# Weight sums of a seven-product scheme: two of four made by adding transfers, in another order of products

## The chip, the cores and the metric

The kernel runs on one core of a Trainium2 chip. The metric is the device time of one execution in microseconds. TensorE (PE) does the matrix products, VectorE (DVE) and ScalarE (ACT) the elementwise work, GpSimd (POOL) has so far little to do, and SyncE (SP) issues the transfers.

## The reference, cut to what matters

One decoder layer runs on 512 prompt tokens and 64 sample tokens (576 in all, model width 2048):

```
c = rms_norm(x) @ w_in                      # 2048 x 10312: q, k, v, z_attn, indexer, GLU, z_conv, two gates
attn -> branch_attn = (attn * silu(z_attn)) @ w_up_attn          # 1024 x 2048
u = glu_val * sigmoid(glu_gate); dw = depthwise_conv(u, 31 taps)
conv_out = silu(layer_norm(dw)) @ w_pw + b_pw
branch_conv = (conv_out * silu(z_conv)) @ w_up_conv              # 1024 x 2048
merged = sigmoid(gate_attn) * branch_attn + sigmoid(gate_conv) * branch_conv
y = rms_norm(x + merged @ w_out)
```

All data is float32. The change lies in how a part of `x @ w_in` and the whole of `attn @ w_up_attn` are multiplied.

## The kernel before

**Split products.** A float32 weight tile is split by `split` (L160) into a rounded high part (ACT, `whi`, L164) and the rest (DVE, `wlo`, L166). Activations are kept as such two parts too, and each product takes three matmuls: high by high, high by low, low by high. `whi` and `wlo` have three buffers each, so the splits run up to three tiles ahead of PE.

**Plain blocks.** `block` (L238) makes one strip of 128 output channels for all 576 tokens.

**Pairs with seven products.** `strassen` (L169) makes two strips at once, ca and cb. The contraction is cut in two halves, the 576 tokens in two halves of 288, and the two strips are the two halves of the outputs: a two-by-two scheme in which seven products take the place of eight. The weight quarters are b11 (first half of the rows, strip ca), b12 (first half, cb), b21 and b22 (second half). The weight operands are b11, t1 = b12 - b11, t2 = b22 - t1, b22, b21, b22 - b12 and b21 - t2, each of which goes through `split`. The activation operands (A11, A12, A22, S1 to S4) are made once per stage: L944 to L964 for x, L1081 to L1107 for the attention. The order of products is A11, S1, S2, S4, A12, S3, A22. The results are added up from PSUM by DVE into four kept tiles (`sk`), and `ev` gets each finished quarter.

There are 20 pairs with `w_in` (contraction 2048, so quarter tiles of 128x1024; L982, L992, L998), and 8 with `w_up_attn` (contraction 1024, tiles of 128x512; L1135). One pair has 7 x 24 or 7 x 12 matmuls of 288 columns.

**Buffers.** b11 and b12 come from tag `wraw` (two buffers, shared with the plain blocks), b21 and b22 from `wx` (two), t1 and t2 from `wt` (two). One pair thus fills every buffer of the three tags.

**Order of the work.** The order on each engine is not the source's: a planner simulates the engines with its own costs when the kernel is built and takes, of what it thinks is ready, the lowest priority level (`pri`): weight loads, sums and splits 0, evictions 1, preparation and normalisation 3, convolution taps 5, products 6. Each engine and each queue then runs its list in order and waits where an operand is late. SP's queue has the loads and stores; POOL's queue issues only gathers, and POOL computes small scalings and differences, all before 560 us.

**Stages.** Attention, indexer and plain blocks of `w_in` run up to about 660 us; the 20 pairs of `w_in` up to 1120, with the depthwise convolution's taps (L725) and the layer norm (L1012) beside them on DVE; then the plain blocks of `w_pw` and the first pairs of `w_up_attn`; then pairs and plain blocks of `w_up_conv` by turns; and last `w_out` with the final norm.

Of the kernel before, what the change touches and what calls it, by code (L numbers as in the profile page):

```python
# [9 lines left out]
F32 = mybir.dt.float32  # L10
# [4 lines left out]
OP = mybir.AluOpType  # L15
# [70 lines left out]
def build(tc, I, O):  # L86
    nc = tc.nc
    v, s, g, pe = nc.vector, nc.scalar, nc.gpsimd, nc.tensor
    dma = nc.sync.dma_start
# [3 lines left out]
    @contextmanager  # L93
    def pri(level):
        old = tc.cur_priority
        start = level * 1000000 + count.get(level, 0)
        tc.cur_priority = start
        yield
        count[level] = count.get(level, 0) + tc.cur_priority - start
        tc.cur_priority = old  # L100

    def ap(h, off, dims):
        return bass.AP(tensor=h.tensor, offset=h.offset + off, ap=[list(d) for d in dims])

    per = ctx.enter_context(tc.tile_pool(name="per", bufs=1))
# [54 lines left out]
    def split(raw, n=128):  # L160

        k = raw.shape[1]
        hi = per.tile([128, 8, 128], R, name="whi", tag="whi", bufs=3)[:, :k, :n]
        s.copy(hi, raw[:, :, :n])  # L164
        lo = per.tile([128, 8, 128], R, name="wlo", tag="wlo", bufs=3)[:, :k, :n]
        v.tensor_sub(lo, raw[:, :, :n], hi.bitcast(F32))  # L166
        return hi, lo

    def strassen(pool, w, width, ca, cb, A, ev, kts=16, lvl=6, EV=1, rp=None):  # L169


        n = kts // 2
        with pri(0):
            raws = []
            for c0, half, tag in ((ca, 0, "wraw"), (cb, 0, "wraw"), (ca, 1, "wx"), (cb, 1, "wx")):
                t = (per.tile([128, 8, 128], F32, name="wraw", tag="wraw", bufs=2) if tag == "wraw" else
                     (rp or pool).tile([128, 8, 128], F32, name="wx", tag="wx", bufs=2))[:, :n]
                dma(t, ap(w, half * n * 128 * width + c0, [[width, 128], [128 * width, n], [1, 128]]))
                raws.append(t)
            b11, b12, b21, b22 = raws  # L180
            t1 = pool.tile([128, n, 128], F32, name="t1", tag="wt", bufs=2)
            t2 = pool.tile([128, n, 128], F32, name="t2", tag="wt", bufs=2)

        def product(raw, x):
            p = ps.tile([128, 512], F32, name="mms", tag="mm", bufs=4)[:, :T2]
            with pri(0):
                hi, lo = split(raw)
            with pri(lvl):
                for k in range(n):
                    for j, (a, part) in enumerate(((hi, 0), (hi, 1), (lo, 0))):  # L190
                        pe.matmul(p, a[:, k], A[x](part, k), start=(k == 0 and j == 0), stop=(k == n - 1 and j == 2))  # L191
            return p

        def kept():
            return pool.tile([128, T2], F32, name="sk", tag="sk", bufs=5)

        k1, k5, u2, v2 = (kept() for _ in range(4))

        def add(out, a, b):
            with pri(EV):  # L200
                v.tensor_add(out, a, b)  # L201

        p = product(b11, "A11")
        with pri(EV):
            s.copy(k1, p)  # L205
        with pri(0):
            v.tensor_sub(t1, b12, b11)
        p = product(t1, "S1")
        with pri(EV):
            s.copy(k5, p)  # L210
        with pri(0):
            v.tensor_sub(t2, b22, t1)
        p = product(t2, "S2")
        add(u2, p, k1)
        p = product(b22, "S4")
        with pri(0):
            v.tensor_sub(b22, b22, b12)
        add(v2, u2, k5)
        add(v2, p, v2)
        with pri(EV):  # L220
            ev(0, 1, v2)
        p = product(b21, "A12")
        with pri(0):
            v.tensor_sub(b21, b21, t2)
        add(k1, p, k1)
        with pri(EV):
            ev(0, 0, k1)
        p = product(b22, "S3")
        add(u2, p, u2)
        add(k5, u2, k5)  # L230
        with pri(EV):
            ev(1, 1, k5)
        p = product(b21, "A22")
        add(u2, p, u2)
        with pri(EV):
            ev(1, 0, u2)

    def block(w, width, c0, x, n=128, kts=16, lvl=6, hs=(0, 1), units=None):  # L238

        p = {h: ps.tile([128, 512], F32, name=f"mm{h}", tag="mm", bufs=4) for h in hs}  # L240
        for u in range(kts // 8):
            hi, lo = units[u] if units else weight_unit(w, width, c0, n, u * 8)
            with pri(lvl):
                for k in range(8):
                    kt = u * 8 + k
                    for j, (a, part) in enumerate(((hi, 0), (hi, 1), (lo, 0))):
                        for h in hs:
                            pe.matmul(p[h][:n, :HN[h]], a[:, k, :n], x(part, kt, h),  # L248
                                      start=(kt == 0 and j == 0), stop=(kt == kts - 1 and j == 2))
        return p  # L250
# [29 lines left out]
    def xrows(i):  # L280
        return (ap(I["x_prompt"], i * 128 * D, [[D, 128], [1, D]]) if i < 4
                else ap(I["x_sample"], 0, [[D, 64], [1, D]]))

    with tc.tile_pool(name="p0", bufs=1) as p0, pri(-1):
# [11 lines left out]
        def load(i):  # L296
            for cs in (slice(0, D // 2), slice(D // 2, D)):
                dma(xt[i][:TILES[i][1], cs], xrows(i)[:, cs])  # L298
# [27 lines left out]
        for h, tiles in enumerate(((0, 1), (2, 3, 4))):  # L326
            for i in tiles:
                n = TILES[i][1]
                for k, (eng, c0, c1) in enumerate(SQ[i]):
                    x, out = xt[i][:n, c0:c1], ss[:n, i, k:k + 1]  # L330
# [7 lines left out]
            with pri(-2):  # L338
# [13 lines left out]
                for c0, c1, eng in SCALE if h else ():  # L352
                    for k, i in enumerate(tiles):
                        x = xt[i][:TILES[i][1], c0 * 128:c1 * 128]
                        n = TILES[i][1]
                        (g if eng == "P" else v).tensor_scalar(x, x, rr[:n, k:k + 1], rt[:n, k:k + 1],
                                                               op0=OP.mult, op1=OP.mult)
            for kt in range(16):
                tag = PT_TAGS[h][kt % len(PT_TAGS[h])]
                pt = ps.tile([128, 512], F32, name="pt", tag=tag, bufs={"mm": 4, "w": 3, "o": 1}[tag])  # L360
                for i in tiles:
                    t0, n = TILES[i]
# [12 lines left out]
        for q in range(4):  # L375
            rows = slice(q * 32, (q + 1) * 32)
# [12 lines left out]
    CH, TK, EV = 3, 5, 1  # L389
# [31 lines left out]
    p = block(I["w_in"], D_IN, C_KI, xin, 72, units=units)  # L421
# [12 lines left out]
    with pri(CH):  # L434
# [15 lines left out]
        wt = p1.tile([128, 4, 8], F32, name="wt", tag="qh", bufs=2)  # L450
# [17 lines left out]
    for c in range(4):  # L468
        p = ps.tile([128, 512], F32, name="mm1", tag="mm", bufs=4)
# [8 lines left out]
        with pri(EV):  # L478
            s.copy(qi[:, c], p[:, NW:NQ])
            for e in range(2):  # L480
                rows = slice(e * 64, (e + 1) * 64)
# [107 lines left out]
    for kv in range(2):  # L589
        p = win(C_K + 128 * kv)  # L590
# [9 lines left out]
    for kv in range(2):  # L600
        p = win(C_V + 128 * kv)
# [15 lines left out]
    for h in range(NH):  # L617
        p = win(C_Q + 128 * h)
# [318 lines left out]
    def whole(dst, q, c):  # L937
        v.tensor_add(dst, q.bitcast(F32)[:, 0, c], q.bitcast(F32)[:, 1, c])
# [5 lines left out]
    with pri(CH):  # L944
        for q in range(4):
            c = slice(2 * q, 2 * q + 2)
            fs = [p4.tile([128, 2, T2], F32, name="f", tag="f", bufs=4) for _ in range(4)]
            whole(fs[0], quarter(1, 0), c)
            whole(fs[1], quarter(1, 1), c)
            v.tensor_add(fs[1], fs[0], fs[1])  # L950
            whole(fs[2], quarter(0, 0), c)
            parts(s1, fs[1], c)
            v.tensor_sub(fs[2], fs[1], fs[2])
            whole(fs[3], quarter(0, 1), c)
            parts(s2, fs[2], c)
            v.tensor_sub(fs[3], fs[3], fs[2])
            parts(s4, fs[3], c)
        for q in range(4):
            c = slice(2 * q, 2 * q + 2)
            f0, f1 = (st("f").rearrange("p (k t) -> p k t", k=2) for _ in range(2))  # L960
            whole(f0, quarter(0, 0), c)
            whole(f1, quarter(1, 0), c)
            v.tensor_sub(f0, f0, f1)
            parts(quarter(1, 0), f0, c)  # L964
# [47 lines left out]
    with pri(CH):  # L1012
        ones = p5.tile([128, 128], F32, name="ones")
        v.memset(ones, 1.0 / 1024)
        for h in range(2):
            sl, n = TS2[h], T2
# [42 lines left out]
        for k in range(0, 8, 2):  # L1059
            for h, x in ((0, back), (1, dw)):  # L1060
                t = x[:, k:k + 2]
# [19 lines left out]
    with pri(CH):  # L1081
        for k in range(4):
            t1, t2 = st("al"), st("al")
            dma(t1, a_d[k])
            dma(t2, a_d[k + 4])
            x11, x21, x12, x22 = t1[:, TS2[0]], t1[:, TS2[1]], t2[:, TS2[0]], t2[:, TS2[1]]

            def put(name, src):
                o = UA[name]
                s.copy(o[:, 0, k], src)  # L1090
                v.tensor_sub(o[:, 1, k], src, o.bitcast(F32)[:, 0, k])

            def new():
                return pU.tile([128, T2], F32, name="sk", tag="sk", bufs=5)

            f1, f2, f3, f4 = (new() for _ in range(4))
            put("A11", x11)
            v.tensor_sub(f3, x11, x21)
            put("S3", f3)
            v.tensor_add(f1, x21, x22)  # L1100
            put("S1", f1)
            v.tensor_sub(f2, f1, x11)
            put("S2", f2)
            put("A12", x12)
            put("A22", x22)
            v.tensor_sub(f4, x12, f2)
            put("S4", f4)  # L1107
    XU = {a: (lambda part, k, o=o: o[:, part, k]) for a, o in UA.items()}
    cT = per.tile([128, 2, 8, T], R, name="cT", tag="x1")
# [86 lines left out]
    for h in (1, 0):  # L1196
# [42 lines left out]
        for j in range(16):  # L1239
            p = block(I["w_out"], D, 128 * j, mx, hs=(h,))  # L1240
# [6 lines left out]
        with pri(EV):  # L1247
# [3 lines left out]
            r, t = rsqrt(p2, tot, [128, 3], "f", last=False)  # L1251
# [48 lines left out]
```

## Time and profile before

| | |
|---|---|
| median of 3 runs | 1603.06 us (1602.15 to 1606.78) |
| profiled execution | 1603.4 us, span 1601.3 us |
| granted TensorE clock, mean | 0.994 |
| PE busy | 1565.7 us (98%), 11506 matmuls |
| DVE busy | 1186.3 us (74%) |
| ACT busy | 696.1 us (43%) |
| POOL busy | 53.7 us (3%) |
| DMA, mean | 143 GB/s |

A busy share is an average over stages. Where PE is busy all the time, what the other engines do costs nothing; where PE has gaps, the question is which engine's work it waited for. Matmuls overlap, so PE's busy time is less than count times mean duration.

### The profile page before, as it was taken

The numbers are of one execution on the slowest core, as the hardware profiler recorded it, in microseconds if no ns is written. First come the engines' busy times: TensorE is split into PE (matmuls) and PEld (weight loads), VectorE is DVE, ScalarE is ACT, GpSimd is POOL, SyncE is SP. The second block draws the span as 40 slices with busy tenths as digits, with TensorE's granted clock in tenths as the row PEclk, the third lists the DMA queues.
The fourth block names the chain that finished last, engine by engine and source line by source line (L and its number), as shares of the span: only waits on it lengthen the run. The fifth ranks groups of instructions, "written<-read, shape, count | busy, mean of one in ns | idle before, by whom it ended". The sixth has DMA issues, their size and how long they took to land.

```text
span 1601.3 us, 28533 instructions
## 1 busy us (share of the span) xinstructions
PE 1565.7 (98%) x11506; PEld 1520.8 (95%) x11506; DVE 1186.3 (74%) x2049; ACT 696.1 (43%) x1169; POOL 53.7 (3%) x73
## 2 busy tenths in 40 slices
PE   7999999999999999999999999999999999999997
PEld 6889999899989999999999999999989999999996
DVE  5436996365849599999999999999877675445554
ACT  5444324535455432344343345657533232334443
POOL 2200100101110000000000000000000000000000
PEclk9999999999999999999999999999999999999998
DMA  6632534434444334344343453644655665855763
GB/s 197 186 109 67 176 109 125 136 104 129 131 140 118 87 85 119 106 115 121 91 122 94 143 156 112 182 120 133 198 176 173 191 212 183 255 161 145 209 199 106
DMA packets 323827, 228.96 MB, mean 143 GB/s; under 512 B 15317, under 2 KB 293973, under 8 KB 322976
## 3 DMA queue, kind: packets, MB, share of 16 engines
q1 hardware_dynamic: 321008, 217.71, 46.4%
q0 software_dynamic: 2688, 9.44, 1.8%
q8 instruction: 90, 1.47, 0.4%
q14 instruction: 41, 0.34, 0.1%
HBM read 193.53 MB, written 36.96 MB: 144 GB/s over the span
## 4 chain that ended last, share of the span: by engine, by line
PE 87%; DVE 7%; DMA 3%; issue 1%; ACT 1%; SPq 1%; POOL 0%; ACTq 0%; DVEq 0%; POOLq 0%
PE mm L248 49%; PE mms L191 27%; PE mm L476 2%; DVE wlo L166 2%; PE po L805 1%; DMA wraw<-in_w_in 1%; PE po L874 1%; PE pw L787 1%; DVE dw L725 1%; DMA wx<-in_w_pw 1%; PE pw L801 1%; PE pw L1218 1%; PE pw L536 1%; DVE sk L201 0%; SPq L298 0%
## 5 line engine op out<-in xcount | busy, mean ns | idle before, releaser
L248 PE MATMUL mm<-x,whi 128*128 128x256 f32 (+2 forms) x2368 | 430.2, 297 | 0.5 <-DVE x L371 0.4
L248 PEld LDWEIGHTS mm<-x,whi 128*128 128x128 f32 (+1 forms) x2368 | 358.0, 186 | 6.8 <-issue 3.9
L164 ACT CAST whi<-wraw 128x1024 fp32r<-128x1024 f32 (+2 forms) x154 | 157.4, 1023 | 282.4 <-PE mm L248 205.4
L248 PE MATMUL mm<-x,wlo 128*128 128x256 f32 (+3 forms) x1184 | 260.0, 296 | 0.0
L191 PE MATMUL mms<-x,whi 128*128 128x288 f32 x1280 | 255.4, 296 | 4.2 <-ACT sk L210 1.6
L166 DVE TENSOR_TENSOR wlo<-wraw,whi 128x1024 fp32r<-128x1024 f32 (+2 forms) x154 | 183.3, 1190 | 88.9 <-ACT whi L164 88.1
L164 ACT CAST whi<-wx 128x1024 fp32r<-128x1024 f32 (+1 forms) x156 | 150.1, 962 | 200.3 <-PE mm L248 55.6
L166 DVE TENSOR_TENSOR wlo<-wx,whi 128x1024 fp32r<-128x1024 f32 (+1 forms) x156 | 173.2, 1111 | 63.4 <-ACT whi L164 62.8
L191 PEld LDWEIGHTS mms<-x,whi 128*128 128x128 f32 x1280 | 204.6, 189 | 5.9 <-ACT sk L210 2.1
L248 PE MATMUL mm<-m,whi 128*128 128x320 f32 (+1 forms) x1024 | 207.9, 298 | 0.0
L248 PEld LDWEIGHTS mm<-x,wlo 128*128 128x128 f32 (+1 forms) x1184 | 198.1, 186 | 0.7 <-issue 0.2
L191 PE MATMUL mms<-s,whi 128*128 128x288 f32 x960 | 191.6, 295 | 1.3 <-ACT sk L205 0.8
L191 PE MATMUL mms<-x,wlo 128*128 128x288 f32 x640 | 187.8, 297 | 3.9 <-DVE wlo L166 3.8
L725 DVE SCALAR_TENSOR_TENSOR dw<-u,cp,dw 128x512 f32<-128x512 f32 x240 | 178.0, 748 | 1.5
L248 PEld LDWEIGHTS mm<-m,whi 128*128 128x128 f32 x1024 | 164.2, 189 | 0.0
L191 PEld LDWEIGHTS mms<-s,whi 128*128 128x128 f32 x960 | 153.2, 188 | 1.9 <-ACT sk L205 1.0
L248 PE MATMUL mm<-m,wlo 128*128 128x320 f32 (+1 forms) x512 | 151.2, 296 | 0.0
L191 PE MATMUL mms<-s,wlo 128*128 128x288 f32 x480 | 140.7, 296 | 0.0
L191 PEld LDWEIGHTS mms<-x,wlo 128*128 128x128 f32 x640 | 120.0, 189 | 5.6 <-DVE wlo L166 5.5
L164 ACT CAST whi<-t 128x1024 fp32r<-128x1024 f32 (+1 forms) x56 | 52.0, 928 | 106.2 <-PE mm L248 56.2
L248 PEld LDWEIGHTS mm<-m,wlo 128*128 128x128 f32 x512 | 96.4, 188 | 0.0
L191 PEld LDWEIGHTS mms<-s,wlo 128*128 128x128 f32 x480 | 89.9, 188 | 0.5 <-DVE wlo L166 0.4
(320 smaller groups left out, 2282.7 us busy)
## 6 DMA issues: line engine op xcount, KB each, us to landing
wraw<-in_w_in SPq DMA_DIRECT2D x120, 512.0 KB
wx<-in_w_in SPq DMA_DIRECT2D x40, 512.0 KB
wraw<-in_w_out SPq DMA_DIRECT2D x32, 512.0 KB
wx<-in_w_out SPq DMA_DIRECT2D x32, 512.0 KB
ga<-ga_d SPq DMA_DIRECT2D x32, 288.0 KB
ga_d<-gt SPq DMA_DIRECT2D x16, 288.0 KB
gc_d<-gt SPq DMA_DIRECT2D x16, 288.0 KB
gc<-gc_d SPq DMA_DIRECT2D x16, 288.0 KB
```

Source lines behind the costliest of these rows:

```text
L164: s.copy(hi, raw[:, :, :n])
L166: v.tensor_sub(lo, raw[:, :, :n], hi.bitcast(F32))
L191: pe.matmul(p, a[:, k], A[x](part, k), start=(k == 0 and j == 0), stop=(k == n - 1 and j == 2))
L248: pe.matmul(p[h][:n, :HN[h]], a[:, k, :n], x(part, kt, h), start=(kt == 0 and j == 0), stop=(kt == kts - 1 and j == 2))
L476: pe.matmul(p[:, :NQ], a[:, k], xk(part, kt)[:, 128:], start=(kt == 0 and j == 0), stop=(kt == 15 and j == 2))
L536: pe.matmul(d0[:, :W], qdup(part, h)[:, (i - 1) * 128:i * 128], kst[:, :W], start=(part == 0), stop=(part == 1))
L725: v.scalar_tensor_tensor(o1, a1, k1, o1, op0=OP.mult, op1=OP.add)
L787: pe.matmul(S[:, :max(W, 256)], a, x[:, kv, :max(W, 256)], start=(j == 0), stop=(j == 2))
L801: pe.transpose(pt[:, b * 128:(b + 1) * 128], Lt[:, b * 128:(b + 1) * 128], ident)
L805: pe.matmul(out[:, i * 128:(i + 1) * 128], vt[:, b, kv * 128:(kv + 1) * 128], PT[:, b * 128:(b + 1) * 128], start=(b == 0), stop=(b == i))
L874: pe.matmul(out[q:q + 32, :128], PT[:, r, q:q + 32], vc[:, b2, r * 256 + kv * 128:r * 256 + kv * 128 + 128], start=(r == 0), stop=False, t ...
L1218: pe.transpose(pt[:n, i * 128:(i + 1) * 128], yt[:, o:o + n], ident)
```

## The change

The sums change sign so that they can be made by adding alone. One tile t takes the place of t1 and t2 and grows: it is loaded with b12, and an adding transfer issued by POOL (`more_of`, `accum_op=OP.add`) adds b11, read from memory a second time (product S1); DVE adds b22 in place (S2) and later b21 (A22). An adding transfer adds b12 into b22 after S4's split (S3). So DVE makes two weight sums per pair where it made four, and POOL issues two adding transfers. The order of products is A11, S1, S4, S2, A12, S3, A22. `wraw` now holds b11 and b21, `wx` b22 alone, `wt` t alone. The operands S1 and S4 change sign, and with them some additions of the results.

```diff
-            raws = []
-            for c0, half, tag in ((ca, 0, "wraw"), (cb, 0, "wraw"), (ca, 1, "wx"), (cb, 1, "wx")):
-                t = (per.tile([128, 8, 128], F32, name="wraw", tag="wraw", bufs=2) if tag == "wraw" else
-                     (rp or pool).tile([128, 8, 128], F32, name="wx", tag="wx", bufs=2))[:, :n]
-                dma(t, ap(w, half * n * 128 * width + c0, [[width, 128], [128 * width, n], [1, 128]]))
-                raws.append(t)
-            b11, b12, b21, b22 = raws
-            t1 = pool.tile([128, n, 128], F32, name="t1", tag="wt", bufs=2)
-            t2 = pool.tile([128, n, 128], F32, name="t2", tag="wt", bufs=2)
+            b11 = load(shape(per, "wraw"), 0, ca)
+            t = load(shape(pool, "wt", n), 0, cb)
+            more_of(t, 0, ca)
+            b22 = load(shape(rp or pool, "wx"), 1, cb)
+            b21 = load(shape(per, "wraw"), 1, ca)
...
+        def rows(half, c0):
+            return ap(w, half * n * 128 * width + c0, [[width, 128], [128 * width, n], [1, 128]])
+        def load(tile, half, c0):
+            dma(tile, rows(half, c0))
+            return tile
+        def more_of(tile, half, c0):
+            with pri(0):
+                g.dma_start(out=tile, in_=rows(half, c0), accum_op=OP.add)
...
         p = product(b11, "A11")
         with pri(EV):
             s.copy(k1, p)
+        p = product(t, "S1")
         with pri(0):
-            v.tensor_sub(t1, b12, b11)
-        p = product(t1, "S1")
+            v.tensor_add(t, t, b22)
         with pri(EV):
             s.copy(k5, p)
+        p = product(b22, "S4")
+        more_of(b22, 0, cb)
+        add(v2, p, k5)
+        p = product(t, "S2")
         with pri(0):
-            v.tensor_sub(t2, b22, t1)
-        p = product(t2, "S2")
+            v.tensor_add(t, t, b21)
         add(u2, p, k1)
-        p = product(b22, "S4")
-        with pri(0):
-            v.tensor_sub(b22, b22, b12)
-        add(v2, u2, k5)
-        add(v2, p, v2)
+        sub(v2, v2, u2)
         with pri(EV):
             ev(0, 1, v2)
         p = product(b21, "A12")
-        with pri(0):
-            v.tensor_sub(b21, b21, t2)
         add(k1, p, k1)
         with pri(EV):
             ev(0, 0, k1)
         p = product(b22, "S3")
         add(u2, p, u2)
-        add(k5, u2, k5)
+        sub(k5, k5, u2)
...
-        p = product(b21, "A22")
+        p = product(t, "A22")
...
-            v.tensor_add(fs[1], fs[0], fs[1])
+            v.tensor_sub(fs[1], fs[0], fs[1])
...
-            v.tensor_sub(fs[3], fs[3], fs[2])
+            v.tensor_add(fs[3], fs[3], fs[2])
...
-            v.tensor_add(f1, x21, x22)
+            v.tensor_sub(f1, x21, x22)
...
-            v.tensor_sub(f4, x12, f2)
+            v.tensor_add(f4, x12, f2)
```

## Rows read from the trace of the kernel before

**Rows 1.** The page's first part: busy time, share and instructions of each engine.

```profile
PE 1565.7 (98%) x11506; PEld 1520.8 (95%) x11506; DVE 1186.3 (74%) x2049; ACT 696.1 (43%) x1169; POOL 53.7 (3%) x73
```

**Rows 2.** Stretches: us, then busy PE, PEld, DVE, ACT, POOL; clock, DMA, GB/s.

```profile
660.00:900.00 240.00, 230.61 (x1706) 226.45 (x1705) 233.74 (x315) 95.18 (x134) 0.00 (x0) 1.00 0.38 109
780.00:900.00 120.00, 113.80 (x835) 110.82 (x834) 116.92 (x158) 46.60 (x66) 0.00 (x0) 1.00 0.38 109
...
900.00:1120.00 220.00, 220.00 (x1653) 219.56 (x1653) 203.70 (x294) 126.21 (x193) 0.00 (x0) 1.00 0.48 140
1120.00:1220.00 100.00, 94.71 (x679) 92.04 (x679) 75.93 (x162) 43.07 (x87) 0.00 (x0) 0.98 0.58 181
1220.00:1300.00 80.00, 80.00 (x602) 79.75 (x601) 58.92 (x108) 24.18 (x39) 0.00 (x0) 1.00 0.62 191
```

**Rows 3.** TensorE's waits, 600 to 900 us: total us, times, longest us.

```profile
PE mms L191 <- DVE wlo L166: 3.8, 6, 1.1
PE mms L191 <- ACT sk L210: 1.6, 2, 0.8
PE mms L191 <- ACT whi L164: 1.6, 3, 0.6
PE mms L191 <- DVE x L942: 1.4, 1, 1.4
```

**Rows 4.** TensorE's waits, 1100 to 1300 us.

```profile
PE mm L248 <- ACT whi L164: 2.5, 3, 1.3
PE mms L191 <- DVE wlo L166: 1.6, 3, 0.7
```

**Rows 5.** The chain that ended last, 780 to 800 us: start us, us.

```profile
786.57 1.14 DVE wx L217
...
789.82 1.13 DVE wx L224
...
794.88 1.14 DVE t L207
...
797.04 1.15 DVE wlo L166
```

**Rows 6.** Groups on DVE by form, 600 to 1300 us: busy us, mean ns, idle before.

```profile
L725 DVE SCALAR_TENSOR_TENSOR dw<-u,cp,dw 128x512 f32<-128x512 f32 x131 | 96.1, 745 | 0.1
...
L217 DVE TENSOR_TENSOR wx<-wx,wraw 128x1024 f32<-128x1024 f32 x20 | 24.4, 1219 | 0.1
...
L207 DVE TENSOR_TENSOR t<-wraw 128x512 f32<-128x512 f32 x8 | 5.5, 690 | 1.8 <-DMA wraw<-in_w_up_attn 1.7
```

**Rows 7.** The gathers into tile vc: POOL's ns min/median/max, and issue to landing.

```profile
L417 POOL DMA_INDIRECT vc<-in_cache_v,idx x8: 941/950/1947, 159.9 to 469.7; - x8
...
DMA to landing us min/median/max: 5.1/5.4/5.8
```

**Rows 8.** The page's DMA queues: packets, MB, share of 16 engines' span.

```profile
q1 hardware_dynamic: 321008, 217.71, 46.4%
```

**Rows 9.** SP's timeline, 900 to 932 us: a pair's first load and the next pair's.

```profile
908.08 0.38 SPq L178 DMA_DIRECT2D wraw<-in_w_in  x1
...
930.06 0.38 SPq L178 DMA_DIRECT2D wraw<-in_w_in  x1
```

**Rows 10.** ACT's timeline in a large pair: third split's cast, copy of S1.

```profile
921.90 1.05 ACT L164 CAST whi<-t 128x1024 fp32r<-128x1024 f32 x1 [0.77 <-DVE t L212]
...
927.54 0.39 ACT L210 COPY sk<-mms 128x288 f32<-128x288 f32 x1
```

**Rows 11.** DVE's timeline there: the third split's low half.

```profile
923.40 1.22 DVE L166 TENSOR_TENSOR wlo<-t,whi 128x1024 fp32r<-128x1024 f32 x1
```

**Rows 12.** DVE's timeline in a small pair: the third split's low half.

```profile
1253.33 0.69 DVE L166 TENSOR_TENSOR wlo<-t,whi 128x512 fp32r<-128x512 f32 x1
```

**Rows 13.** The chain there: the seven products of that pair.

```profile
1252.71 11.14 PE mms L191 x84
```

**Rows 14.** ACT's timeline there: the third split's cast.

```profile
1252.52 0.62 ACT L164 CAST whi<-t 128x512 fp32r<-128x512 f32 x1 [5.78 <-PE mm L248]
```

More of the change, by code (lines that the diff above doesn't have):

```diff
@@ L172, in strassen, with shape @@
         n = kts // 2
-        with pri(0):
-            raws = []
-            for c0, half, tag in ((ca, 0, "wraw"), (cb, 0, "wraw"), (ca, 1, "wx"), (cb, 1, "wx")):
-                t = (per.tile([128, 8, 128], F32, name="wraw", tag="wraw", bufs=2) if tag == "wraw" else
-                     (rp or pool).tile([128, 8, 128], F32, name="wx", tag="wx", bufs=2))[:, :n]
-                dma(t, ap(w, half * n * 128 * width + c0, [[width, 128], [128 * width, n], [1, 128]]))
-                raws.append(t)
-            b11, b12, b21, b22 = raws
-            t1 = pool.tile([128, n, 128], F32, name="t1", tag="wt", bufs=2)
-            t2 = pool.tile([128, n, 128], F32, name="t2", tag="wt", bufs=2)
+        def rows(half, c0):
[6 more added lines that the diff above has]
+                g.dma_start(out=tile, in_=rows(half, c0), accum_op=OP.add)
+        def shape(p, tag, k=8):
+            return p.tile([128, k, 128], F32, name=tag, tag=tag, bufs=2)[:, :n]
+        with pri(0):
+            b11 = load(shape(per, "wraw"), 0, ca)
[3 more added lines that the diff above has]
+            b21 = load(shape(per, "wraw"), 1, ca)
         def product(raw, x):
@@ L201, in add, with sub @@
                 v.tensor_add(out, a, b)
+        def sub(out, a, b):
+            with pri(EV):
+                v.tensor_sub(out, a, b)
         p = product(b11, "A11")
```

## The prediction

> **What bounds the kernel now.** I read the page's first line, then the stretches, then TensorE's waits, then the chain of one bad stretch, then the clock marks of one pair. The first line has PE busy for 1565.7 of 1601.3 us [rows 1], and the number of products is unchanged, so nothing but PE's idle time can be won. The seven-product pairs run from about 660 us on. By stretches [rows 2] PE is idle for 240 - 230.61 = 9.4 us from 660 to 900, of which 120 - 113.80 = 6.2 us from 780 on; for nothing from 900 to 1120; for 5.3 us from 1120 to 1220; for nothing after. That makes 14.7 us, or 0.9%, the most that the change can bring. Where PE idles, DVE is full: 233.74 of 240 us from 660 to 900, 116.92 of 120 from 780 on. But DVE at 204 of 220 us from 900 to 1120 costs PE nothing, so a lower DVE share is worth something only where DVE comes last. TensorE's waits [rows 3] say that it does: the low halves of the weights (wlo, L166), then copies and casts of ACT. The chain from 781 to 798 us [rows 5] shows why: three weight sums of 1.13 to 1.14 us (L217, L224, L207) stand in one run of DVE work that ends in the low half for which PE waits. From 1120 to 1220 the waits [rows 4] are mixed: 2.5 us for a cast of a plain block's weights, 1.6 us for low halves of the pairs.
>
> **The change, part by part.** *Sums.* There are 28 pairs, 20 with 128x1024 tiles (L207, L212, L217 and L224 each x20) and 8 with 128x512 tiles. Four DVE sums per pair become two: 2 x 1.22 = 2.44 us less per large pair, 2 x 0.69 = 1.38 us per small one [rows 6], 49 and 11 us in all. Beside busy PE that is worth nothing; on the path it is worth the idle time that it removes. From 780 to 900 two of the three sums in the chain go (2.3 us), and the longest single wait there is 1.1 us, so I take the whole 6.2 us. Before 780, 3.2 us are idle; 1.4 of them wait for S3's own operand (L942) [rows 3], which the change leaves; I take 1.8. In 1120 to 1220 I take the 1.6 us of rows 4 and leave the cast, which a late load of a plain block holds. Relief: 9.6 us; bounds 0 (the planner fills the freed time with other DVE work) and 14.7.
>
> *Evictions.* The other signs of S1 and S4 turn some additions into subtractions of the same shape: seven DVE operations of 128x288 per pair before and after. The operand preparation (L950, L956, L1100, L1106) likewise changes sign only. Both cost nothing, with no cover needed.
>
> *Loads.* SP issues four loads per pair as before. POOL, which is idle in these stretches, issues two adding transfers: one reads 128x1024 again into t, the other adds b12 into b22. That is 20 x 2 x 0.52 + 8 x 2 x 0.26 = 25 MB more from HBM. The main queue's 217.71 MB took 46.4% of 1601.3 us [rows 8], 293 GB/s, so 0.52 MB takes 1.8 us of all engines. A pair lasts 930.06 - 908.08 = 22.0 us [rows 9]; two transfers of 1.8 us each, or 3.6 if the destination is read too, add 0.16 to 0.33 to a DMA share of 0.48 [rows 2]. It stays under 1.
>
> *How long an adding transfer takes* the trace doesn't show. The nearest row is the gather of 512 KB (128 rows of 4 KB): 5.4 us from issue to landing, of which POOL's own part is 0.95 us [rows 7]. An adding transfer has 1024 rows of 512 B. Low end: 5.4 us, with the rows and the second read hidden. High end: 5.4 + 1.8 for reading the destination + 7 x 0.95 if POOL's time goes by rows = 13.9 us. I take 5.4 + 1.8 + 0.95 = 8.2 us, near the gather, since the engines can move rows while POOL still writes the later ones. At 256 KB the same steps give 4.5, 8.3 and 5.8 us.
>
> The Trainium skill (Collectives: The Full Stack, "The bandwidth ceiling: the fold count and why AG ≠ RS ≠ AR") says that an add in the DMA engines needs two source reads and runs at about half the rate of a copy. By that rule the second read is paid in full, as in the value taken; by the gather's row alone the values would be 6.4 and 4.9 us, and the sum 4.0 us lower, 1593.8. No run here shows it yet.
>
> *What t waits for.* t has two buffers, so the next pair's t can be loaded once A22 of the pair before the present one is split. Nine splits later, 9 x 22.0 / 7 = 28 us, S1 needs it. Load and adding transfer in series are under 2 x 13.9 = 27.8 us even at the high end: hidden (13.6 us at the value taken), no cost.
>
> *What b22 waits for.* This is the new wait. b22 may be added to once S4, now third, is split, and S3, sixth, splits the sum. For a large pair: the third split ends at 923.40 + 1.22 = 924.6 us; S1's product ends when its copy starts, 927.54 [rows 10, 11]; three products of 3.14 us later, at 937.0, PE wants the sixth, whose split takes 1.05 + 1.22 = 2.3 us and must start by 934.7. The transfer has 10.1 us. It takes 8.2: hidden. For a small pair: the third split ends at 1253.33 + 0.69 = 1254.0 [rows 12]; the seven products start at 1252.71 and take 11.14 us, 1.59 each [rows 13], so the sixth starts at 1260.7 and its split (0.62 + 0.69) by 1259.4 [rows 12, 14]. The transfer has 5.3 us and takes 5.8: 0.5 us late in 8 pairs, 4.0 us. Bounds: 0, and at the high end (13.9 - 10.1) x 20 + (8.3 - 5.3) x 8 = 100 us. While S3's cast waits, ACT's evictions and sigmoids are queued behind it, and behind the low half DVE's additions and the convolution taps; PE waits for both once its four PSUM tiles are full.
>
> Sum: -6.2 - 1.8 - 1.6 + 4.0 = -5.6 us on the profiled execution's 1603.4 us (its span 1601.3 and 2.1 around it): 1597.8 us. The median before is 1603.06, 0.3 us lower, which I leave aside.
>
> **The rivals.** *All idle time goes*: the adding transfers are hidden everywhere and the loads, now a pair ahead, also free the casts: 1603.4 - 14.7 = 1588.7. For it: t and b22 now have two buffers each. Against: 2.5 us of the waits are for a plain block's load.
>
> *The relief is refilled*: DVE's order is planned ahead, and 131 convolution taps of 0.745 us [rows 6] are there to fill any gap, so DVE stays full and the same splits come last; with the 4.0 us of the small pairs the time is 1603 to 1607. For it: DVE is full wherever PE idles. Against: the chain of rows 5 holds the sums themselves.
>
> *b22's transfer is late (slower)*: it is one mechanism, POOL's time per row, and decides from a landing of 10.1 us in large pairs. At 11.5 and 7.0 us it costs 1.4 x 20 + 1.7 x 8 = 42 us, less 9.6: 1635. For it: the only rows on POOL's queue are gathers with an eighth of the rows. Against: nothing but that those gathers are cheap.
>
> *POOL is stretched while DVE is busy*: the same gather kept POOL between 0.94 and 1.95 us [rows 7], and DVE is over 90% busy here. With 1.0 us more the transfers take 9.2 and 6.8 us: still hidden in large pairs, (6.8 - 5.3) x 8 = 12 us in small ones in place of 4, 1605.8 in all. Against: most of those gathers took 0.95. The Trainium skill (SBUF — State Buffer, "Who interferes with whom") has a rule that speaks for it: GpSimd shares a port pair with DVE, and one of the two is blocked while an operation of the other holds what it needs; a DVE operation with two SBUF inputs takes the read side. The spread of rows 7 agrees with a block of that kind without proving it.
>
> *It doesn't do what it says*: the planner may put S3's split so late or A22's so early that the order of products is another than the source's. Then the window is longer, and the case falls to the first two.
>
> **How the numbers follow.** A measurement of this kernel tells some 0.3%, 4.8 us, from no change. The forecast, 1593 to 1602: 0.40. All idle time: 0.10. Refilled: 0.10. Stretched: 0.07. Late: 0.33, spread from 1608 to 1690 with more than half below 1640. The forecast's own range crosses the border of 1598.3, so 0.31 of its 0.40 counts as faster: faster 0.31 + 0.10 = 0.41, same 0.09 + 0.10 + 0.07 = 0.26, slower 0.33. The range goes from 1589 to 1640: it leaves out about 0.04 below and 0.14 above.
>
> **What would show it.** In the profile after: DVE's busy time 60 us lower; PE idle from 780 to 900 under 1 us; two adding transfers per pair on POOL's queue landing in about 8 and 6 us; small pairs with a short wait of PE for S3's weights. A wait of PE for S3 in each large pair, or a landing above 10 us, makes the forecast wrong on the slow side; idle time from 780 to 900 that stays, with DVE still full, makes the relief wrong.

## The result, and the profile after

The changed kernel takes 1619.17 us (median of 4, 1617.25 to 1623.98), the kernel before on the same chip 1603.68 us (1602.15 to 1606.78). The ratio is 1.0097 with a 95% interval of 1.0079 to 1.0114: slower by about 1%, where 1597.8 was forecast. The profiled execution took 1623.98 us (span 1622.2), the upper end of its runs, so differences of the two traces are some 5 us larger than those of the medians.

I read the page of the changed kernel first: busy times, then the DMA queues (packets, MB, share of 16 engines' span), then two of its DMA issues (xcount, KB each, median us from issue to landing).

```profile
PE 1574.9 (97%) x11506; PEld 1530.1 (94%) x11506; DVE 1134.5 (70%) x1993; ACT 696.1 (43%) x1169; POOL 136.3 (8%) x129
...
q1 hardware_dynamic: 321008, 217.71, 46.3%
q0 software_dynamic: 52736, 34.61, 14.7%
...
wt<-in_w_in POOLq DMA_DIRECT2D x20, 512.0 KB, 6.8
wx<-in_w_in POOLq DMA_DIRECT2D x20, 512.0 KB, 6.4
```

The change does what it says. DVE has 56 instructions and 51.8 us less than before [rows 1] (60 were forecast), and POOL's queue lands two adding transfers per large pair in 6.4 and 6.8 us. Next the stretches of [rows 2], in the changed kernel (same columns):

```profile
660.00:900.00 240.00, 238.89 (x1796) 238.05 (x1795) 224.92 (x311) 102.40 (x142) 32.41 (x21) 1.00 0.79 159
780.00:900.00 120.00, 120.00 (x907) 119.99 (x906) 111.50 (x153) 50.50 (x70) 16.30 (x11) 1.00 0.82 166
900.00:1120.00 220.00, 213.34 (x1568) 211.60 (x1567) 172.89 (x260) 119.75 (x185) 26.23 (x17) 0.98 0.79 171
1120.00:1220.00 100.00, 91.72 (x642) 89.22 (x641) 70.61 (x150) 40.47 (x82) 10.21 (x8) 0.95 0.74 195
1220.00:1300.00 80.00, 73.64 (x517) 71.78 (x515) 45.19 (x85) 21.64 (x38) 8.96 (x7) 0.96 0.76 191
```

The relief came where it was forecast: from 780 to 900 PE is idle for nothing and runs 907 matmuls where it ran 835, and over 660 to 900 it is 90 ahead. From 900 on it is given back: 85 fewer up to 1120 (1568 for 1653), then 642 for 679 and 517 for 602. Where the time is lost in the end is read from two marks on PE's timeline (start, us, engine, line), the last matmul of a `w_in` product and the first one of `w_out`, here in the kernel before and then in the changed one:

```profile
1123.14 0.30 PE L191 MATMUL mms<-x,wlo 128*128 128x288 f32 x1
...
1375.63 0.46 PE L248 MATMUL mm<-m,whi 128*128 128x320 f32 x2
```

```profile
1121.87 0.30 PE L203 MATMUL mms<-x,wlo 128*128 128x288 f32 x1
...
1396.53 0.46 PE L261 MATMUL mm<-m,whi 128*128 128x320 f32 x2
```

When the large pairs end, the changed kernel is 1.3 us ahead. The stretch between the marks, with the 8 small pairs and the plain blocks, grows from 252.5 to 274.7 us. After it both need 225.7 us. So the large pairs gave back what they had won, and the stretch of the small pairs lost 22 us. Some of the 22 belong to this one execution, which was slower than the median: in the kernel that changes the small pairs alone (second experiment), whose profiled run is its median, the stretch takes 268.4 us, 15.9 more than before.

What PE waits for (us in total, times, longest) in the changed kernel, first 600 to 1120, then 1120 to 1360:

```profile
PE mms L203 <- ACT whi L164: 5.7, 2, 3.8
PE mms L203 <- DVE wlo L166: 1.6, 2, 0.9
...
PE mms L203 <- ACT whi L164: 12.0, 7, 3.0
PE mm L261 <- ACT whi L164: 3.9, 1, 3.9
```

The low halves on DVE, first in [rows 3] with 3.8 us, are down to 1.6; a cast on ACT stands in their place. The chain of one small pair (start, us, what) and ACT's timeline there (idle time before, and what ended it, in brackets) say which cast:

```profile
1240.00 8.08 DMA wx<-in_w_up_attn
...
1248.17 0.63 ACT whi L164
...
1248.85 3.36 PE mms L203 x16
```

```profile
1248.17 0.62 ACT L164 CAST whi<-wx 128x512 fp32r<-128x512 f32 x1 [6.23 <-DMA wx<-in_w_up_attn]
```

It is S3's: b22's adding transfer, issued behind S4's split, lands 8.08 us later, ACT has stood idle for 6.23 us, and PE had been out of work for 3.01 us when its product began. The forecast's window (from the end of S4's split, when the transfer may start, to the latest start of S3's) was 5.3 us, which gives 8.1 - 5.3 = 2.8 us. Six of the eight small pairs wait for this cast, 11.6 us in all. The same step costs time in two large pairs, here in the chain, the earlier one with PE's first matmul after it:

```profile
983.57 9.15 DMA wx<-in_w_in
...
993.92 0.53 PE L203 MATMUL mms<-x,whi 128*128 128x288 f32 x2 [3.80 <-ACT whi L164]
...
1055.40 11.84 DMA wx<-in_w_in
...
1067.35 1.05 ACT whi L164
...
1068.42 1.24 DVE wlo L166
...
1069.70 2.53 PE mms L203 x9
```

The earlier transfer took 9.15 us, less than the forecast's window of 10.1, and PE still waited 3.80 us, so that window was about 9.15 - 3.80 = 5.4 us: the window is not the same in every pair. Both transfers run beside the layer norm's bulk transfers; that these stretched them is argued from the coincidence and was not tried.

The waits cost more than their length. Stretches of 20 us in the changed kernel (columns of [rows 2]): two around the waits of the large pairs with one without a wait between them, and four with small pairs:

```profile
980.00:1000.00 20.00, 16.20 (x109) 15.82 (x108) 12.88 (x20) 10.23 (x17) 1.56 (x1) 0.91 1.10 258
1020.00:1040.00 20.00, 20.00 (x151) 19.89 (x151) 18.13 (x29) 11.80 (x16) 3.08 (x2) 1.00 0.86 172
1060.00:1080.00 20.00, 17.34 (x118) 16.88 (x117) 10.15 (x13) 6.72 (x9) 1.54 (x1) 0.91 0.76 167
...
1180.00:1200.00 20.00, 17.23 (x115) 16.52 (x114) 12.54 (x25) 6.46 (x12) 2.54 (x2) 0.91 0.72 191
1220.00:1240.00 20.00, 17.51 (x115) 16.61 (x114) 11.78 (x24) 6.60 (x14) 2.30 (x3) 0.91 0.70 175
1240.00:1260.00 20.00, 16.99 (x115) 16.54 (x114) 10.84 (x20) 5.04 (x9) 2.83 (x3) 0.91 0.79 188
1300.00:1320.00 20.00, 18.52 (x126) 18.25 (x127) 11.33 (x22) 5.00 (x7) 0.00 (x0) 0.91 0.54 170
```

Against the 151 of the undisturbed stretch the two large-pair ones lack 42 and 33 matmuls, 75 of the 85 that PE fell behind from 900 to 1120. The four small-pair stretches are idle for 2.8 + 2.5 + 3.0 + 1.5 = 9.8 us, but they do 36 + 36 + 36 + 25 = 133 matmuls less than 151 each, which at 20/151 us are 17.6 us. The first of them cut into pieces of 4 us shows where the rest went:

```profile
1184.00:1188.00 4.00, 3.57 (x26) 3.33 (x26) 3.73 (x8) 1.58 (x4) 0.00 (x0) 1.00 1.03 231
1188.00:1192.00 4.00, 1.66 (x11) 1.19 (x10) 1.04 (x3) 1.56 (x3) 0.00 (x0) 1.00 0.60 168
1192.00:1196.00 4.00, 4.00 (x20) 4.00 (x21) 4.00 (x9) 1.15 (x2) 0.00 (x0) 0.57 0.66 195
1196.00:1200.00 4.00, 4.00 (x33) 4.00 (x32) 3.08 (x7) 0.62 (x1) 1.27 (x1) 1.00 0.67 175
```

PE has its wait up to 1192 us (1.66 of 4 us busy). From 1192 to 1196 it is busy all the time, but the granted clock is 0.57, near the lower of its two levels (1.2 GHz, half of 2.4), and 20 matmuls run where 33 do in the next piece.

### The profile page after: what moved, and what is told of

Read it like the earlier page. It is cut to its first block, busy times and chain, and to the rows that moved or that the text cites. A ratio compares the mean times of both kernels' runs of the same rounds, so it can differ in the third digit from the quotient of the medians.

```text
span 1622.2 us, 28685 instructions
## 1 busy us (share of the span) xinstructions
PE 1574.9 (97%) x11506; PEld 1530.1 (94%) x11506; DVE 1134.5 (70%) x1993; ACT 696.1 (43%) x1169; POOL 136.3 (8%) x129
## 3 DMA queue, kind: packets, MB, share of 16 engines
q0 software_dynamic: 52736, 34.61, 14.7%
## 4 chain that ended last, share of the span: by engine, by line
PE 77%; DMA 10%; DVE 6%; issue 4%; ACT 2%; SPq 0%; POOL 0%; ACTq 0%; DVEq 0%; POOLq 0%
PE mm L261 46%; PE mms L203 21%; DMA wx<-in_w_up_attn 4%; PE mm L489 2%; DMA wx<-in_w_in 2%; DVE wlo L166 2%; ACT whi L164 1%; PE po L818 1%; PE po L887 1%; PE pw L800 1%; DMA wraw<-in_w_in 1%; DMA wt<-in_w_in 1%; DVE dw L738 1%; PE pw L814 1%; PE pw L1231 1%
## 5 line engine op out<-in xcount | busy, mean ns | idle before, releaser
L164 ACT CAST whi<-wraw 128x1024 fp32r<-128x1024 f32 (+2 forms) x182 | 183.4, 1008 | 312.7 <-PE mm L261 208.5
L166 DVE TENSOR_TENSOR wlo<-wraw,whi 128x1024 fp32r<-128x1024 f32 (+2 forms) x182 | 213.2, 1172 | 93.3 <-ACT whi L164 92.5
L164 ACT CAST whi<-wx 128x1024 fp32r<-128x1024 f32 (+1 forms) x100 | 98.2, 982 | 239.9 <-PE mm L261 93.9
L166 DVE TENSOR_TENSOR wlo<-wx,whi 128x1024 fp32r<-128x1024 f32 (+1 forms) x100 | 113.7, 1137 | 114.0 <-ACT whi L164 113.7
L164 ACT CAST whi<-wt 128x1024 fp32r<-128x1024 f32 (+1 forms) x84 | 78.0, 929 | 92.0 <-PE mms L203 57.1
L166 DVE TENSOR_TENSOR wlo<-wt,whi 128x1024 fp32r<-128x1024 f32 (+1 forms) x84 | 89.7, 1068 | 15.0 <-ACT whi L164 14.5
```

## The experiments

All were timed against the kernel before. The theory after the result (W): b22's adding transfer is late for S3, the product that needs it, so the price depends on the time between S4's split and S3. The rival (T): it is the traffic, 25 MB more, that slows other loads and casts. A third theory (O) was that the planner's other order near 1120 us drags on. The first three expectations set W against T and O, the later ones W against T.

**The change in the large pairs alone.** The 8 small pairs call a copy of the old function, and their activation operands keep the old signs.

```diff
-        strassen(pU, I["w_up_attn"], D, 128 * j, 128 * (j + 1), XU, ev, kts=8, rp=p2)
+        strassen_dve(pU, I["w_up_attn"], D, 128 * j, 128 * (j + 1), XU, ev, kts=8, rp=p2)
```

> The 20 large pairs as in the changed kernel, the 8 small pairs (w_up_attn) as before: four sums on DVE, the old product order and operand signs. Theory W (the small pairs wait in each pair for b22's adding transfer): all of the loss lies in the small pairs; w_out's first product, 20.9 us later in the changed kernel, comes 1 to 3 us earlier than before the change or level with it: 1599 to 1605 us. Rival T (the second reading of the weights loads the DMA engines in both stages): part of the loss stays, 1607 to 1613. Rival O (the planner's other order at the stage change near 1120 us, where the changed kernel is 2.2 us late, drags on): 1606 to 1610.

Measured: 1605.21 us, ratio 1.0005 (0.9996 to 1.0014), at the upper edge of W's range. The large pairs' change comes out at nothing: what is won up to 900 us goes in the two late transfers (5.6 us of PE's waits for casts of `whi`, 2 times).

**The change in the small pairs alone.** The 20 large pairs use the old function and the old signs.

```diff
-        strassen(pU, I["w_up_attn"], D, 128 * j, 128 * (j + 1), XU, ev, kts=8, rp=p2)
+        strassen_add(pU, I["w_up_attn"], D, 128 * j, 128 * (j + 1), XU, ev, kts=8, rp=p2)
```

> The reverse: the 20 large pairs as before, the 8 small pairs as in the changed kernel. W: the whole loss, 1618 to 1626 us, with PE idle some 17 us more than before between 1120 and 1360 us and nothing lost before 1120. T: half of it or less, 1606 to 1612, since the large pairs carry five sixths of the added traffic. O: near 1620 if the order of the small pairs is what costs, so this run does not tell O from W.

Measured: 1619.69 us, 1.0094 (1.0079 to 1.011): the whole loss. PE's waits from 1120 to 1360, and the landing of the adding transfers into `wx` (1120 to 1400), in this kernel:

```profile
PE mms L272 <- ACT whi L164: 12.0, 7, 5.2
...
DMA to landing us min/median/max: 4.5/5.8/8.5
```

With 4.2 MB more in place of 25, and the same 12.0 us of waits, the amount of traffic is not what counts. From 1120 to 1360 PE is idle for 10.3 us more than before, not for the 17 expected, and does 119 matmuls fewer, which at 20/151 us are 15.8 us.

**S3's operand in a tile of its own, small pairs.** The free half of b22's buffer is loaded with b22 again and gets b12 ahead of time. The adding transfers stay, one load per pair comes on top, S3 no longer waits for S4's split.

```diff
-            b22 = load(shape(rp or pool, "wx"), 1, cb)
+            both = (rp or pool).tile([128, 8, 128], F32, name="wx", tag="wx", bufs=2)
+            b22 = s3 = load(both[:, :n], 1, cb)
+            if n == 4:
+                s3 = load(both[:, 4:], 1, cb)
+                more_of(s3, 0, cb)
...
-        more_of(b22, 0, cb)
+        if n == 8:
+            more_of(b22, 0, cb)
...
-        p = product(b22, "S3")
+        p = product(s3, "S3")
```

> The changed kernel, but in the small pairs S3's operand has a tile of its own (the free half of b22's buffer): b22 is loaded there a second time and b12 added to it ahead of the pair, so the adding transfer waits for no split. One load of 256 KB more per small pair. W: the waits of PE behind S3's cast in the small pairs go and the time comes back to 1599 to 1606 us. T: more traffic than in the changed kernel, so 1619 to 1624 us. O: the order of products is the changed one, so 1616 or more.

Measured: 1607.01 us, 1.0015 (1.0006 to 1.0023), 12 us under the changed kernel with more traffic than it, and 1 us above W's range. PE's waits for S3's cast in the small pairs are gone, so they were most of the cost; T and O had 1616 or more. What stays in this stage is 6.2 us of PE's waits for evictions of `w_pw`'s blocks (`zc`), which come back below.

**Two sums left out.** The kernel before without the subtractions at L217 and L224; their part of the result is missing.

```diff
-        with pri(0):
-            v.tensor_sub(b22, b22, b12)
...
-        with pri(0):
-            v.tensor_sub(b21, b21, t2)
```

> The kernel before with two of the four DVE sums left out in every pair (b22 - b12 and b21 - t2; the products take b22 and b21 as loaded, so that part of the computation is missing). It measures what the relief of DVE alone is worth, with no adding transfer. Forecast's own term: -9.6 us, 1592 to 1596 us, with PE idle under 1 us from 780 to 900 us. Rival (the planner refills the freed time with convolution taps): 1600 to 1605.

Measured: 1584.94 us, 0.9881 (0.9866 to 0.9896). The relief alone is worth 19 us, twice the forecast's term; 12.5 us of it are won before the last `w_in` product. It is a stand-in for the change, which moves L217 and, in place of L224, L207 of the same shape. Two stretches of it (columns of [rows 2]):

```profile
660.00:780.00 120.00, 119.57 (x901) 119.33 (x900) 114.85 (x162) 52.12 (x73) 0.00 (x0) 1.00 0.40 111
780.00:900.00 120.00, 119.48 (x901) 119.23 (x900) 113.28 (x155) 49.83 (x71) 0.00 (x0) 1.00 0.41 116
```

From 780 to 900 PE gains 5.7 us of busy time but 66 matmuls, which at 120/901 us are 8.8 us.

**One adding transfer.** t's stays. S3's operand is made by DVE from t: after b22 is added to it, t holds b11 + b12 + b22, so S3's b12 + b22 is t - b11. Three sums on DVE.

```diff
-        more_of(b22, 0, cb)
+        with pri(0):
+            v.tensor_sub(b22, t, b11)
```

> The changed kernel with one adding transfer per pair instead of two: t is still loaded and added to ahead of the pair, but S3's operand is made by DVE out of tiles that are there (t after b22 was added, less b11, equals b12 + b22). Three DVE sums per pair, no split waits for a transfer that starts inside its own pair. Theory W (what costs is the wait for b22's transfer inside the pair): no such wait left, and half of the 19 us that leaving two sums out was worth: 1592 to 1599 us. Rival T (adding transfers cost by their traffic, whatever waits for them): half of the changed kernel's loss against the relief stays, (1619 - 1585) / 2 above 1585, so 1600 to 1606 us.

Measured: 1596.85 us, 0.9952 (0.9938 to 0.9965), with no wait of over 0.5 us for a cast of a pair's weights.

**One adding transfer, large pairs alone.** The same edit, with the old function in the small pairs.

```diff
-        more_of(b22, 0, cb)
+        with pri(0):
+            v.tensor_sub(b22, t, b11)
...
-        strassen(pU, I["w_up_attn"], D, 128 * j, 128 * (j + 1), XU, ev, kts=8, rp=p2)
+        strassen_dve(pU, I["w_up_attn"], D, 128 * j, 128 * (j + 1), XU, ev, kts=8, rp=p2)
```

> One adding transfer per pair in the 20 large pairs as in the one-transfer kernel, the 8 small pairs as before the change. Tells the stages of that kernel apart. W: the large pairs alone bring half of the 12.5 us that leaving two sums out brought before 1120 us: 1596 to 1600 us. T: 1602 to 1608 us.

Measured: 1598.66 us, 0.997 (0.9959 to 0.9982). t's transfer, which PE never waits for, wins on its own; the small pairs add little to it.

**A tile of its own in all pairs.** As in the third experiment, with b22 loaded a second time for the large pairs too.

```diff
-            b22 = load(shape(rp or pool, "wx"), 1, cb)
+            both = (rp or pool).tile([128, 8, 128], F32, name="wx", tag="wx", bufs=2)
+            b22 = s3 = load(both[:, :n], 1, cb)
+            s3 = load(both[:, 4:] if n == 4 else shape(rp or pool, "wx"), 1, cb)
+            more_of(s3, 0, cb)
...
-        more_of(b22, 0, cb)
...
-        p = product(b22, "S3")
+        p = product(s3, "S3")
```

> S3's operand gets a tile of its own in all 28 pairs (large pairs: the second buffer of b22's tag, so b22 is no longer loaded a pair ahead): loaded once more and added to ahead of its split. Two DVE sums per pair as in the changed kernel, one more load of 512 or 256 KB per pair. W: no transfer is started by a split and awaited three products later; 1588 to 1600 us. T: three more MB-sized transfers' worth per two pairs on DMA engines that are 0.76 to 0.88 busy already from 660 to 1000 us: loads come late everywhere, 1612 to 1640 us.

Measured: 1598.65 us, 0.9965 (0.9951 to 0.9979), 20 us under the changed kernel though it reads most; T had 1612 or more. The last matmul of a `w_in` product stands at 1111.0 us, level with 1110.7 in the kernel with two sums left out: with no transfer late, the large pairs get the whole relief. What is left are three waits of PE, 6.0 us, for DVE's evictions of `w_pw`'s blocks (`zc`, L1133), which themselves wait for the load of `zc` (10.2 us, 3 times).

**S3 last.** S3 goes behind A22: one product more between S4's split and S3, and one more addition of 128x288. All sums, loads and transfers stay.

```diff
+        p = product(t, "A22")
+        w2 = kept()
+        add(w2, p, u2)
         p = product(b22, "S3")
         add(u2, p, u2)
+        add(w2, p, w2)
         sub(k5, k5, u2)
         with pri(EV):
             ev(1, 1, k5)
-        p = product(t, "A22")
-        add(u2, p, u2)
-        with pri(EV):
-            ev(1, 0, u2)
+            ev(1, 0, w2)
```

> The changed kernel with S3 as the last product, after A22 (one more 128x288 addition per pair on DVE): b22's transfer has one product more time, 1.6 us in small pairs and 3.1 us in large ones. W: transfers of the small pairs land in 4.4 to 8.7 us (median 6.3) against 5.3 us before and 6.9 us here, so about two thirds of the small pairs' loss goes, and the two late ones of the large pairs with it: 1600 to 1609 us. T: nothing changes, 1617 to 1622 us.

Measured: 1595.57 us, 0.9947 (0.9933 to 0.9961), the lowest time of a complete kernel here (the ratio with one adding transfer, 0.9952, lies within its interval): 23.6 us under the changed one by the place of S3, and the order that the planner makes of it. PE's waits in it, 600 to 1120 and then 1120 to 1360, and last the landing of the small pairs' adding transfers into `wx`, 1120 to 1400:

```profile
PE mms L203 <- DVE wlo L166: 1.7, 3, 1.2
PE pw L1042 <- PE mms L203: 0.7, 1, 0.7
PE mms L203 <- ACT whi L164: 0.3, 1, 0.3
...
PE mm L262 <- ACT whi L164: 2.6, 1, 2.6
...
PE mms L203 <- ACT whi L164: 0.7, 1, 0.7
...
DMA to landing us min/median/max: 5.0/5.9/7.0
```

The pairs' products wait 1.0 us for casts where they waited 17.7. T had 1617 or more here, and falls. The time is also 4 us under W's range, which reckoned with the changed kernel's slow landings (8.7 us against a window of 6.9): in this order none takes over 7.0. Why they are quicker was not tried.

**S3 last, and a tile of its own in the small pairs.** The edit is that of the last experiment with that of the third.

```diff
-            b22 = load(shape(rp or pool, "wx"), 1, cb)
+            both = (rp or pool).tile([128, 8, 128], F32, name="wx", tag="wx", bufs=2)
+            b22 = s3 = load(both[:, :n], 1, cb)
+            if n == 4:
+                s3 = load(both[:, 4:], 1, cb)
+                more_of(s3, 0, cb)
...
-        p = product(b22, "S3")
+        p = product(t, "A22")
+        w2 = kept()
+        add(w2, p, u2)
+        p = product(s3, "S3")
...
```

> The changed kernel with S3 moved behind A22 in all 28 pairs, and in the 8 small pairs also S3's operand loaded and added in a tile of its own, so that its adding transfer can run a pair ahead (0.26 MB more per small pair). With S3 last alone the time was 1595.57 us and the small-pair stage (last w_in product to first w_out product) took 254.2 us, against 247.4 us with two sums left out. Window theory: the adding transfer can no longer be late in the small pairs, so some of these 6.8 us come back: 1589 to 1595, and no wait of TensorE there for the cast of S3's operand. Traffic theory: more reads in the stretch with the highest DMA share cost time instead: 1597 or more. If neither, 1595 to 1597, the rest of the stage's loss is DVE's (low halves) and not a transfer's.

Measured: 1602.93 us, 0.999 (0.9978 to 1.0001), with runs from 1597.58 to 1607.56: worse than S3 last alone, and above W's range. No wait for S3 was left to save, and PE's waits from 1110 to 1400 have others; below them the end of the chain behind the longest for `zc`:

```profile
PE mms L207 <- DVE zc L1137: 4.8, 3, 2.8
PE mm L267 <- ACT whi L164: 3.6, 1, 3.6
...
1210.41 4.38 DMA zc<-zc_d
1214.91 0.49 DVE zc L1137
1215.54 16.10 PE mms L207 x108
```

They belong to the plain blocks, and those for `zc` go back to a late load. In the three kernels with a tile of its own in the small pairs DVE waits 9.9 to 10.4 us for the load of `zc`, in the changed kernel 8.7, with S3 last alone 4.8. Whether the reads themselves or the other order of the work cost these 7 us is open; in this one place T's expectation was met.

**S3 one product earlier, large pairs.** From the first experiment, with S3 ahead of A12.

```diff
+        p = product(b22, "S3")
+        add(u2, p, u2)
+        sub(k5, k5, u2)
+        with pri(EV):
+            ev(1, 1, k5)
         p = product(b21, "A12")
...
-        p = product(b22, "S3")
-        add(u2, p, u2)
-        sub(k5, k5, u2)
-        with pri(EV):
-            ev(1, 1, k5)
         p = product(t, "A22")
```

> The kernel with the change in the 20 large pairs alone (1605.21 us), with S3 one product earlier there, ahead of A12; same loads, same sums, same transfers. Window theory: the adding transfer of b22 then has 10.1 - 3.1 = 7.0 us in place of 10.1, against a landing of 6.4 to 6.7 us in the median with tails to 12: late by little in a third to a half of the pairs, and dearer where the granted clock falls after a wait: 1608 to 1622, with waits of TensorE for S3's cast in many large pairs. If the price in the small pairs came from something that belongs to them (their size, the plain blocks between them) and not from the window: 1603 to 1607, no new waits.

Measured: 1628.49 us, 1.016 (1.0146 to 1.0173), 23 us above the first experiment and beyond the upper end of W's range. PE's waits from 600 to 1120:

```profile
PE mms L203 <- ACT whi L164: 19.2, 23, 3.4
```

Three microseconds less of window turn two waits into 23, about half of them for S3's cast itself and most of the others for the splits queued right behind it. The loss follows the window in the large pairs too. The landing's median there is 6.7 us, under the 7.0 that the expectation left it, so the usable window is often shorter than worked out, as in the pair at 983.57 us; what takes the rest was not measured.

Of W's nine ranges four held, one was met at its edge, and four were missed by 1 to 8 us: W names the cause and not the size. Between the two marks the kernels with unchanged small pairs took 252.5 to 257.1 us, and no complete kernel with changed ones took less than 253.7, so what the good orders win lies in the large pairs.

## Why the prediction was wrong

**Right.** Which idle time goes: PE's gaps from 660 to 900, made by DVE. POOL's time does not go by rows: an adding transfer of 1024 rows holds POOL for 1.5 us, not 7 x 0.95, and lands in 6.4 us between the forecast's 5.4 and 8.2. t's transfer is hidden: ACT waited for it once, PE never. b22's is hidden in 18 of 20 large pairs. No row shows a wait for the pairs' evictions. The windows, 10.1 and 5.3 us, tell which kind of pair waits; single pairs had less (about 5.4 us in the large pair at 983.57).

**The step that failed** is "What b22 waits for". For a small pair it had a transfer of 5.8 us, 0.5 us late, 4.0 us in 8 pairs; for a large one "hidden", at nothing. Up to the last `w_in` product the forecast had -6.2 - 1.8 = -8.0 us; measured are -1.3, where leaving two sums out gave -12.5, so the two late transfers took some 11 us (an estimate). From there to `w_out` it had -1.6 + 4.0 = 2.4 us; measured are 22.2 (15.9 in the second experiment). The landing there, of the adding transfers into `wx` in the changed kernel, 640 to 900 and then 1120 to 1400 us:

```profile
DMA to landing us min/median/max: 6.2/6.4/8.3
...
DMA to landing us min/median/max: 4.4/6.3/8.7
```

At best half the bytes land 1.8 us sooner, near the 2.4 us that I took; in the median they land no sooner. In the example at 1240 us the issue stood right behind t's adding transfer on POOL's queue, at 1238.97. Where the median is over the window by 1.0 us and the tail by 3.4, a typical duration should not have been the term: the wait is one-sided, early landings give nothing back. Landing times also moved with the order of the work (5.8 and 5.9 us in the median, at most 8.5 and 7.0, in the second experiment and with S3 last), so no single figure would have held. And I gave an idle microsecond the price of one, where with the fall of the granted clock it cost 1.8 (17.6 for 9.8) in the changed kernel and 1.5 (15.8 for 10.3) in the second experiment. As an estimate, 12.0 us of waits at these prices are 18 to 22 us.

**The relief** was mis-sized the other way: 9.6 us against the 19 of the kernel with two sums left out. I took PE's idle time for the most that could be won, 14.7 us. Busy time in a stretch with waits holds fewer matmuls per microsecond; 835 in [rows 2] against 901 (1653 in 220 us, also in [rows 2], give the same rate) would have said 8.8 us where I wrote 6.2. That this miss hid part of the other is luck: with a relief of 9.6 us the loss would have been some 10 us larger.

**The DMA engines.** I forecast 0.16 to 0.33 more of them, for one read or two. From 900 to 1120, the stretch that the forecast started from, the share went from 0.48 to 0.79, within it; from 660 to 900 it went from 0.38 to 0.79, above it. The queues say why. Before, POOL's queue had this line:

```profile
q0 software_dynamic: 2688, 9.44, 1.8%
```

The other 34.61 - 9.44 = 25.2 MB, the adding transfers, took 14.7 - 1.8 = 12.9% of 1622.2 us, 120 GB/s, where q1's transfers ran at 290. Here an add costs 2.4 times a load per byte. The Trainium skill (Collectives: The Full Stack, "The bandwidth ceiling: the fold count and why AG ≠ RS ≠ AR") gives two source reads and about half the rate of a copy for the adding step of a collective. The 2.4 times agree in kind; the landing of the large transfers does not, since 6.4 us is the forecast's value without the second read. On average the engines had room (0.79), though not in the stretch of the 9.15 us landing (1.10 from 980 to 1000), and the experiments with more reads were faster than the change.

**The rivals.** The slower rival named the right place, b22's transfer, with the wrong mechanism (POOL's time per row) and therefore the wrong pairs: it decided in the large ones, and mainly small ones paid. POOL stretched by DVE does not show: from 660 to 900 us, with DVE at 94%, the 11 issues for b22 took 1.53 to 1.57 us, and the 9 from 900 on, with DVE at 79%, took the same. The Trainium skill (SBUF — State Buffer, "Who interferes with whom"), in the section that the prediction names, also infers that a DVE operation with two inputs takes only the read side of the shared ports, while writing a transfer's descriptors needs the write side. These rows agree with that.

## What to carry to other kernels

Where a transfer is started by one step and awaited by a later one, compare the shortest window with the slow landings, not typical values of both, and move the consumer back until it holds them: one place in the order was worth 23.6 us here, more than the 19 that the saved DVE work was worth. Make operands by transfer when nothing on the path starts that transfer, as with t, and by the engine when something does. Size a relief by matmuls per stretch against a clean stretch, not by PE's idle time.

## What was not expected of the hardware

Four waits of PE of 1.8 to 3.0 us were each followed by some microseconds at a lower granted clock (0.57 from 1192 to 1196 us, near the lower level), and cost nearly twice their length in the changed kernel: 133 matmuls (17.6 us) for 9.8 us of idle time. An adding transfer of 256 KB landed there in the median no sooner than one of 512 KB (6.3 against 6.4 us), though at best 1.8 us sooner; in another order of the products it landed in 5.9.
